# Where a filler's steps stand at the ends of the RWKV mixer's pairs of heads

## The chip, the cores and the metric

The kernel runs on 1 core of one Trainium2 chip. The metric is the device time of one execution in microseconds. A core has TensorE (PE in the rows, PEld for its weight loads), VectorE (DVE), ScalarE (ACT), GpSimd (POOL) and SyncE (SP), which issues most of the DMAs. Each engine works through its own queue in the order that the program gives it.

## The reference

Two blocks of a network run over 512 tokens of width 1024. The first mixes the tokens in three branches (RWKV-7, S5, gated linear attention), weighs each with a gate, and goes on to cross-attention and a feed-forward part; the second has attention, a linear recurrence and two more feed-forward parts. The change lies in the RWKV branch, which has 8 heads of width 64. Cut to what matters:

```python
def step(S, inp):                                   # per token and head
    r_t, w_t, k_t, v_t, kk_t, a_t = inp
    sa = jnp.einsum('bhvk,bhk->bhv', S, -kk_t)
    S = (S * w_t[:, :, None, :] + sa[..., None] * (kk_t * a_t)[:, :, None, :]
         + v_t[..., None] * k_t[:, :, None, :])
    return S, jnp.einsum('bhvk,bhk->bhv', S, r_t)
_, y = lax.scan(step, S0, seq)
mean = jnp.mean(y, axis=-1, keepdims=True)
var = jnp.mean(jnp.square(y - mean), axis=-1, keepdims=True)
y = ((y - mean) * lax.rsqrt(var + RWKV_GN_EPS)).reshape(B, L, MIX_W) * ln_w + ln_b
bonus = jnp.sum(r_h * k_h * r_k, axis=-1, keepdims=True) * v_h
y = (y + bonus.reshape(B, L, MIX_W)) * g
...
gates = jax.nn.sigmoid(p_gate).reshape(B, L, N_BRANCH, D_MODEL)
merged = (gates[:, :, 0] * (y_rw @ w_branch[l, 0]) + gates[:, :, 1] * (y_s5 @ w_branch[l, 1])
          + gates[:, :, 2] * (y_gla @ w_branch[l, 2]))
```

## The kernel before

All matrices are multiplied in two parts, a high and a low one: one 128x128 weight block costs three matmuls of 512 columns. A weight tile of 512 KB is loaded by SP (`Stream.load`, L191; three raw buffers), split by ACT (L206) and VectorE (L207) into high and low halves (four buffers of half a tile each), and used.

The RWKV branch treats its 8 heads as four pairs, `hp` 0 to 3, each with 128 features. For a pair it projects k, r and v (`project`, 24 matmuls on L244 each; those of the next pair are traced at three places inside the present one, after the matrices of the pair, after the solve and before the loop). It then makes the pair's *front* (decays, normalised keys, transposes, the products NR, KR and A), *solves* a triangular system in chunks of 64 tokens (five rounds of 64x64 matmuls, L527, each with copies by ACT and sums by VectorE), computes UA, RT, GT and H, and goes through a *loop over chunks* (L719 to L729): each turn multiplies GT by the state, VectorE adds H (L724), and RT times the state gives the chunk's y. Behind the loop stands the *end of the pair*: VectorE adds the y's (L730), a matmul takes each head's mean away (L738, "the means"), ACT squares the result (L740), eight small matmuls sum the squares (L743, a helper on L349, "the sums"), VectorE, GpSimd and VectorE make reciprocal roots, four matmuls broadcast them (L744, on L366), and two more matmuls (L747 bonus, L752 gate) and VectorE finish the pair. The solve of a pair uses the same PSUM banks as the end of the pair before it.

Beside this runs the *filler* (`gates`, L1186): a generator whose every step is three matmuls of 512 columns on L1200. Eight steps make one tile: 16 tiles of gates for the merge of the branches, then 4 tiles of products for S5, 160 steps in all. They accumulate in one PSUM bank of their own; the eighth step of a tile ends with a tanh or a copy by ACT and a store to DRAM (for S5 nine stores, eight of them by SP, L1219). `b.fill(n)` traces the next n steps at its place; `b.fill_behind(ins, n)` traces them there too and makes their TensorE instructions come behind `ins` on TensorE's queue.

The order of every queue is set when the kernel is built. The planner takes, whenever an engine is free in its own reckoning, the instruction traced earliest among those whose operands are ready. So the place where a loose step is traced says only what goes before it when both are ready; a step can run far earlier than its neighbours in the code. For pairs 0 to 2 the code traces 3 steps in the front, 5 before NR, 16 in the solve, 6 in the loop and 2 behind it, 32 a pair, all loose. Pair 3 has 41 loose ones up to its solve and 23 tied ones: two behind each of six turns of the loop, then 3, 3 and 5 behind the last turn, the means and the sums.

Of the kernel before, what the change touches and what calls it, by code (L numbers as in the profile page):

```python
# [23 lines left out]
NCH = 8  # L24
# [452 lines left out]
def rwkv(b, st, xs, Y0, pp, ps, ctx, early):  # L477

    nc, v, c = b.nc, b.v, b.c
# [39 lines left out]
    def ch(t):  # L519
        return t.rearrange("p (c s) -> p c s", s=C64)  # L520

    def mmc(out, lhsT, rhs, cs=range(NCH), start=True, stop=True):

        for ci in cs:
            for a in range(2):
                r = slice(a * 64, a * 64 + 64)
                ins = nc.tensor.matmul(out(r, ci), lhsT(r, ci), rhs(r, ci), start=start, stop=stop)  # L527
        return ins

    def first():  # L530
        return pp.tile([P, 512], F32, tag="ps", name="pp")

    def bank():
        return ps.tile([P, 512], F32, tag="ps", name="ps")
# [3 lines left out]
    def work(name, pool=None):  # L538
        return (pool or w1).tile([P, L], F32, tag=tags.get(name, name), name=name)
# [16 lines left out]
    for hp in range(4):  # L556
# [21 lines left out]
        sq = work("sq")  # L578
        nc.scalar.activation(sq, k, AF.Square, scale=v["rw_k_k"][:, hp : hp + 1])
        b.fill(3)  # L580
        acc = first()
# [132 lines left out]
        y = work("y")  # L714
# [4 lines left out]
        for ci in range(1, NCH):  # L719
            prev = (lambda r, _: H[r, 0]) if ci == 1 else (lambda r, _: S[r, ci])  # L720
            if ci < NCH - 1:
                p = bank()[:, :C64]
                ins = mmc(lambda r, _: p[r], lambda r, _: GT[r, ci], prev, [0])
                nc.vector.tensor_tensor(S[:, ci + 1], H[:, ci], p, op=ALU.add)  # L724
            if hp == 3 and ci < NCH - 1:
                b.fill_behind(ins, 2)
            ins = mmc(lambda r, ci: py[r, ci], prev, lambda r, ci: RT[r, ci], [ci])
            if hp < 3 and ci < NCH - 1:
                b.fill()  # L729
        nc.vector.tensor_tensor(ch(y)[:, 1:], ch(y)[:, 1:], py[:, 1:], op=ALU.add)  # L730


        behind = (lambda ins, n: b.fill_behind(ins, n)) if hp == 3 else (lambda ins, n: None)
        if hp < 3:
            b.fill(2)
        behind(ins, 3)
        pc = bank()
        behind(nc.tensor.matmul(pc, c["cmat"], y, start=True, stop=True), 3)  # L738
        yc, sq = work("yc"), work("sq2")
        nc.scalar.activation(sq, pc, AF.Square)  # L740
        nc.scalar.copy(yc, pc)
        acc = bank()
        behind(b.token_sums(acc, sq, c["hsel"], 4, True, True), 5)  # L743
        rb = b.head_rows(acc[:, :8], ps, w1, 1.0 / 64, 64e-5, ("yr", "y"))  # L744
        nc.vector.tensor_tensor(yc, yc, rb, op=ALU.mult)
        pb = bank()
# [640 lines left out]
def block1(b, st, ctx, c0, context):  # L1387
# [6 lines left out]
    with ExitStack() as mx:  # L1394
# [18 lines left out]
        with ExitStack() as c:  # L1413
            Y0 = b.pool("yr", 1, ctx=c, side="right").tile([P, 4, L], F32, name="Y0")
            with ExitStack() as c1:
                b.filler = gates(b, st, hs, (2, 1), made, b.pool("gate", 1, ctx=c1), b.pool("ps1a", 1, PSUM, ctx=c1))
                rwkv(b, st, hs, Y0, b.pool("ps1p", 2, PSUM, ctx=c1), b.pool("ps1r", 3, PSUM, ctx=c1), c1, pre.make)
                b.drain()
            yp = room("ys")
            y0 = yp()  # L1420
            for k in range(4):
                b.scaled_parts(y0[0][:, k], y0[1][:, k], Y0[:, k], 0.5)
# [846 lines left out]
```

## Time and profile before

| | us |
|---|---|
| median of 3 runs | 3179.24 |
| lowest, highest | 3174.16, 3182.07 |
| the profiled execution's own time | 3181.27 |
| its span, first to last instruction | 3179.5 |
| TensorE busy in it | 3071.8 |
| RWKV's pairs in it | from about 40 to 400 us of the span |

The rows come from the profiled execution, in microseconds from its first instruction. Busy time of matmuls is modelled: they overlap, so the start of one to the start of the next says what one costs. A granted clock of 1.00 is 2.4 GHz, of 0.50 is 1.2 GHz.

### The profile page before, as it was taken

The numbers are of one execution on the slowest core, as the hardware profiler recorded it, in microseconds if no ns is written. First come the engines' busy times: TensorE is split into PE (matmuls) and PEld (weight loads), VectorE is DVE, ScalarE is ACT, GpSimd is POOL, SyncE is SP. The second block draws the span as 40 slices with busy tenths as digits, with TensorE's granted clock in tenths as the row PEclk, the third lists the DMA queues.
The fourth block names the chain that finished last, engine by engine and source line by source line (L and its number), as shares of the span: only waits on it lengthen the run. The fifth ranks groups of instructions, "written<-read, shape, count | busy, mean of one in ns | idle before, by whom it ended". The sixth has DMA issues, their size and how long they took to land.

```text
span 3179.5 us, 51627 instructions
## 1 busy us (share of the span) xinstructions
PE 3071.8 (97%) x20456; PEld 2635.5 (83%) x20456; DVE 1841.7 (58%) x3374; ACT 1247.0 (39%) x2436; POOL 748.5 (24%) x827
## 2 busy tenths in 40 slices
PE   8999899989999999899999999999999999899998
PEld 6888777769797888896669988888999998788888
DVE  6545395556465556777767784323655656653445
ACT  4333234335354334646655221212544444332323
POOL 3322141220030000568765000000322223210002
PEclk9999999999999999999999999999999999999999
DMA  4122233334154332432225473221421111123334
GB/s 141 59 74 65 68 96 90 123 100 139 54 170 143 119 99 84 144 97 81 80 75 166 145 262 98 61 66 58 134 73 54 49 59 47 47 75 98 95 97 120
DMA packets 115938, 310.29 MB, mean 98 GB/s; under 512 B 32352, under 2 KB 37168, under 8 KB 115184
## 3 DMA queue, kind: packets, MB, share of 16 engines
q1 hardware_dynamic: 110480, 294.99, 30.0%
q10 hardware_dynamic: 5216, 12.00, 1.0%
q8 instruction: 161, 2.64, 0.3%
q14 instruction: 81, 0.66, 0.1%
HBM read 296.23 MB, written 9.44 MB: 96 GB/s over the span
## 4 chain that ended last, share of the span: by engine, by line
PE 86%; DVE 8%; issue 2%; POOL 2%; DMA 1%; ACT 1%; SPq 0%; DVEq 0%; POOLq 0%; ACTq 0%
PE acc L244 58%; PE gate L1200 3%; PE ps L527 3%; PE acc L265 2%; PE acc L267 2%; PE acc L266 2%; PE ps L1998 2%; DVE wl L207 2%; PE mods L1508 1%; PE ss L349 1%; PE rstd L425 1%; PE sc L1763 1%; PE st L1784 1%; PE acc L1806 1%; PE st L1785 1%
## 5 line engine op out<-in xcount | busy, mean ns | idle before, releaser
L206 ACT CAST wh<-raw 128x512 fp32r<-128x512 f32 (+1 forms) x899 | 538.1, 604 | 836.5 <-PE acc L244 662.9
L207 DVE TENSOR_TENSOR wl<-raw,wh 128x512 fp32r<-128x512 f32 (+1 forms) x779 | 578.4, 745 | 494.5 <-ACT wh L206 491.3
L244 PE MATMUL acc<-hh,wl 128*128 128x512 f32 (+2 forms) x2264 | 747.7, 363 | 9.3 <-DVE th L1236 4.4
L244 PE MATMUL acc<-hh,wh 128*128 128x512 f32 (+2 forms) x2264 | 747.3, 361 | 0.0
L244 PE MATMUL acc<-hl,wh 128*128 128x512 f32 (+2 forms) x2264 | 746.7, 361 | 0.0
L244 PEld LDWEIGHTS acc<-hh,wl 128*128 128x128 f32 (+1 forms) x2264 | 396.6, 189 | 84.3 <-issue 5.2
L244 PEld LDWEIGHTS acc<-hh,wh 128*128 128x128 f32 (+1 forms) x2264 | 397.3, 189 | 67.4 <-issue 1.9
L244 PEld LDWEIGHTS acc<-hl,wh 128*128 128x128 f32 (+1 forms) x2264 | 396.6, 189 | 63.8 <-issue 0.6
L207 POOL TENSOR_TENSOR wl<-raw,wh 128x512 fp32r<-128x512 f32 (+1 forms) x120 | 142.9, 1193 | 1106.8 <-ACT wh L206 1097.3
L244 PE MATMUL acc<-mh,wl 128*128 128x512 f32 (+1 forms) x848 | 262.2, 335 | 1.2 <-DVE wl L207 0.8
L244 PE MATMUL acc<-mh,wh 128*128 128x512 f32 (+1 forms) x848 | 260.4, 332 | 0.0
L244 PE MATMUL acc<-ml,wh 128*128 128x512 f32 (+1 forms) x848 | 260.2, 331 | 0.1
L244 PEld LDWEIGHTS acc<-mh,wl 128*128 128x128 f32 x848 | 150.5, 188 | 18.3 <-DVE wl L207 1.2
L244 PEld LDWEIGHTS acc<-ml,wh 128*128 128x128 f32 x848 | 150.8, 188 | 17.7 <-DVE ml L343 0.5
L244 PEld LDWEIGHTS acc<-mh,wh 128*128 128x128 f32 x848 | 150.5, 188 | 17.2
L354 POOL TENSOR_TENSOR rs<-rs,ct_all 128x2 f32<-128x2 f32 (+1 forms) x32 | 27.5, 860 | 449.3 <-DVE rs L416 449.3
L265 PE MATMUL acc<-wl,hh 128*128 128x256 f32 x448 | 126.5, 285 | 1.4 <-DVE Xc L1574 1.4
L266 PE MATMUL acc<-wh,hl 128*128 128x256 f32 x448 | 126.6, 284 | 0.0
L267 PE MATMUL acc<-wh,hh 128*128 128x256 f32 x448 | 125.7, 284 | 0.0
L1574 DVE SCALAR_TENSOR_TENSOR X<-acc,mod,X 128x256 f32<-128x256 f32 (+1 forms) x112 | 65.2, 593 | 94.8 <-PE acc L244 94.6
L1622 ACT ACTIVATE t<-acc 128x512 f32<-128x512 f32 x66 | 34.6, 526 | 195.1 <-PE acc L244 195.1
L1794 POOL TENSOR_TENSOR pl<-pr,ph 128x512 fp32r<-128x512 f32 x75 | 103.0, 1382 | 9.4 <-ACT ph L1791 4.5
(604 smaller groups left out, 5826.0 us busy)
## 6 DMA issues: line engine op xcount, KB each, us to landing
raw<-in_ffn_in_dram SPq DMA_DIRECT2D x88, 512.0 KB, 3.6
ada<-in_ada_dram SPq DMA_DIRECT2D x48, 512.0 KB, 3.8
w<-in_ada_dram SPq DMA_DIRECT2D x48, 512.0 KB, 4.5
raw<-in_ffn_w_up_dram SPq DMA_DIRECT2D x44, 512.0 KB, 3.6
raw<-in_ffn_out_dram SPq DMA_DIRECT2D x32, 512.0 KB, 3.5
raw<-in_hg_w_dram SPq DMA_DIRECT2D x32, 512.0 KB, 3.5
raw<-in_ffn_out_dram SPq DMA_DIRECT2D x40, 384.0 KB, 3.1
raw<-in_w_gate_dram SPq DMA_DIRECT2D x24, 512.0 KB, 3.6
```

Source lines behind the costliest of these rows:

```text
L206: nc.scalar.copy(h, x)
L207: (nc.gpsimd if self.help and n else nc.vector).tensor_tensor(l, x, h.bitcast(F32), op=ALU.subtract)
L244: nc.tensor.matmul(z[0], w, z[x], start=k == 0 and n == 0, stop=k == ks - 1 and n == 2)
L265: nc.tensor.matmul(acc, xh, wl, start=k == 0, stop=False)
L266: nc.tensor.matmul(acc, xl, wh, start=False, stop=False)
L267: nc.tensor.matmul(acc, xh, wh, start=False, stop=k == ks - 1)
L527: ins = nc.tensor.matmul(out(r, ci), lhsT(r, ci), rhs(r, ci), start=start, stop=stop)
L1200: nc.tensor.matmul(acc, w, x, start=k + i == 0, stop=k == 7 and i == 2)
L1574: return lambda i, acc: b.nc.vector.scalar_tensor_tensor(X[:, i], acc, gate[:, i : i + 1], X[:, i], op0=ALU.mult, op1=ALU.add)
L1622: nc.scalar.activation(t, a, AF.Tanh, scale=0.5)
L1794: (nc.vector if n % 3 == 1 else nc.gpsimd).tensor_tensor(pl, pr, ph.bitcast(F32), op=ALU.subtract)
L1998: nc.tensor.matmul(p[:, c], kc[:, c * P : (c + 1) * P], qc[:, c * P : (c + 1) * P], start=True, stop=True)
```

## The change

For pairs 0 to 2 the loop traces three loose steps instead of six, one in each of the turns 1, 3 and 5; the two loose steps behind the loop go; two steps are tied behind the means and three behind the sums. A pair still has 32 steps, and pair 3 keeps its ties as they are.

```diff
             ins = mmc(lambda r, ci: py[r, ci], prev, lambda r, ci: RT[r, ci], [ci])
-            if hp < 3 and ci < NCH - 1:
-                b.fill()
+            if hp < 3 and ci % 2:
+                b.fill((1, 1, 1, 0)[ci // 2])
         nc.vector.tensor_tensor(ch(y)[:, 1:], ch(y)[:, 1:], py[:, 1:], op=ALU.add)
 
 
-        behind = (lambda ins, n: b.fill_behind(ins, n)) if hp == 3 else (lambda ins, n: None)
-        if hp < 3:
-            b.fill(2)
-        behind(ins, 3)
+        if hp == 3:
+            b.fill_behind(ins, 3)
         pc = bank()
-        behind(nc.tensor.matmul(pc, c["cmat"], y, start=True, stop=True), 3)
+        b.fill_behind(nc.tensor.matmul(pc, c["cmat"], y, start=True, stop=True), 3 if hp == 3 else 2)
...
         acc = bank()
-        behind(b.token_sums(acc, sq, c["hsel"], 4, True, True), 5)
+        b.fill_behind(b.token_sums(acc, sq, c["hsel"], 4, True, True), 5 if hp == 3 else 3)
```

## Rows read from the trace of the kernel before

**Rows 1.** The page: busy time of engines (share, instructions); a load's us to landing.
```profile
PE 3071.8 (97%) x20456; PEld 2635.5 (83%) x20456; DVE 1841.7 (58%) x3374; ACT 1247.0 (39%) x2436; POOL 748.5 (24%) x827
...
raw<-in_w_gate_dram SPq DMA_DIRECT2D x24, 512.0 KB, 3.6
```

**Rows 2.** Stretches: length, busy time of each engine (instructions), granted clock, DMA share, GB/s.
```profile
270.60:324.40 53.80, 53.49 (x925) 45.72 (x925) 30.04 (x55) 17.09 (x37) 16.07 (x19) 1.00 0.20 61
324.40:341.10 16.70, 11.24 (x83) 7.07 (x77) 3.99 (x12) 1.66 (x3) 1.65 (x1) 0.69 0.01 2
341.10:365.90 24.80, 23.02 (x709) 22.12 (x708) 10.29 (x22) 6.06 (x14) 3.77 (x6) 1.00 0.01 3
```

**Rows 3.** Stretches, the filler's line L1200 alone: its matmuls, then its weight loads.
```profile
40.00:97.50 57.50, 18.19 (x72) 13.31 (x73) 1.00 0.31 97
97.50:181.50 84.00, 30.84 (x120) 21.58 (x120) 1.00 0.21 64
181.50:270.60 89.10, 35.23 (x142) 26.07 (x142) 1.00 0.22 72
270.60:329.50 58.90, 20.49 (x78) 13.85 (x77) 1.00 0.18 56
329.50:365.90 36.40, 0.00 (x0) 0.00 (x0) 0.86 0.01 3
```

**Rows 4.** Timeline of TensorE at pair 0's end.
```profile
181.51 1.10 PE L738 MATMUL ps<-y,ct_mix 128*128 128x512 f32 x2
...
187.49 0.95 PE L349 MATMUL ps<-ct_mix,sq 128*128 128x2 f32 x8
...
195.19 1.05 PE L366 MATMUL hb<-ct_all,hw 128*128 128x128 f32 x8
196.07 1.02 PE L747 MATMUL ps<-rk,bsel 128*128 128x512 f32 x2
```

**Rows 5.** Timeline of TensorE in pair 0's loop (start, duration, engine, line, operation).
```profile
152.28 0.39 PE L1200 MATMUL gate<-hl,wh 128*128 128x512 f32 x1
152.60 0.33 PE L527 MATMUL ps<-S,GT 64*64 64x64 f32 x4
152.97 0.50 PE L1200 MATMUL gate<-hh,wh 128*128 128x512 f32 x1
153.31 0.39 PE L1200 MATMUL gate<-hh,wl 128*128 128x512 f32 x1
153.54 0.40 PE L1200 MATMUL gate<-hl,wh 128*128 128x512 f32 x1
```

**Rows 6.** Timeline of TensorE at pair 2's end, with idle time and what ended it.
```profile
329.57 2.02 PE L738 MATMUL ps<-y,ct_mix 128*128 128x512 f32 x2 [0.79 <-DVE y L730]
332.34 1.86 PE L349 MATMUL ps<-ct_mix,sq 128*128 128x2 f32 x8 [0.75 <-ACT sq L740]
336.74 2.04 PE L366 MATMUL hb<-ct_all,hw 128*128 128x128 f32 x8 [2.54 <-DVE hw L363]
338.58 1.68 PE L747 MATMUL ps<-rk,bsel 128*128 128x512 f32 x2
```

**Rows 7.** Stretches of 3 us at pair 2's end, columns as in rows 2.
```profile
330.00:333.00 3.00, 2.25 (x6) 0.68 (x5) 0.00 (x0) 1.07 (x2) 0.00 (x0) 0.50 0.00 0
...
336.00:339.00 3.00, 2.26 (x9) 2.21 (x10) 0.53 (x2) 0.00 (x0) 0.13 (x1) 0.50 0.00 0
```

**Rows 8.** Loops of pairs 0 and 2: all engines, then twice L527 alone.
```profile
149.00:178.20 29.20, 29.20 (x193) 21.82 (x188) 10.13 (x19) 10.70 (x18) 6.66 (x8) 1.00 0.25 77
...
149.00:178.20 29.20, 3.75 (x86) 2.78 (x80) 1.00 0.25 77
...
324.40:328.70 4.30, 2.92 (x59) 2.06 (x53) 1.00 0.01 3
```

**Rows 9.** Dense work after a fall of the clock, columns as in rows 2.
```profile
690.00:695.00 5.00, 4.85 (x12) 3.83 (x13) 3.07 (x4) 0.63 (x1) 1.66 (x1) 0.51 0.31 97
```

**Rows 10.** Timelines: SP's stores for S5, TensorE in pair 3's loop.
```profile
316.65 5.32 SPq L1219 DMA_DIRECT2D scr<-gate  x8
...
371.96 0.33 PE L527 MATMUL ps<-S,GT 64*64 64x64 f32 x4 [2.10 <-DVE S L724]
```

## The prediction

> **What bounds the kernel now.** I began with the page: TensorE is busy 97% of the span [rows 1]. The change moves no arithmetic, so only three things can alter the time here: TensorE waiting, TensorE at its lower clock, and the small loss each time it passes between 64x64 and 128x128 tiles. Next I read stretches of the mixer. Up to 324.4 us TensorE has no gap worth naming (53.49 of the last 53.80 us busy); from 324.40 to 341.10 it is busy 11.24 of 16.70 us at a granted clock of 0.69, and in the next 24.80 us it is busy 23.02 [rows 2]. I call the four pairs of heads 0 to 3; these two stretches are the loop over chunks and the end of pair 2, and then pair 3's solve.
>
> Why it waits there is in the count of the filler's matmuls (three to a step) [rows 3]. 72+120 = 192 of them, 64 steps, are done when pair 0's means start at 181.51 [rows 4], though only 32 steps are written in the code up to there. At pair 1's means it is 111 against 64, and at pair 2's means 137 against 96. Between 329.5 and 365.9 there is none: what is left are the 23 steps that the code ties behind pair 3's matmuls. So loose steps run whenever TensorE's queue has room, long before the place where they are written, and they are used up when pair 2 ends.
>
> **The change, part by part.** It keeps 32 steps for each of pairs 0 to 2: three loose ones in the loop (there were six, and two behind it), two tied behind the means, three behind the sums of squares. A tie is an order on TensorE's queue and no semaphore; but the filler is one sequence into one PSUM bank, so no later step can pass a tied one. The means of pairs 0, 1 and 2 will then have at most 27, 59 and 91 steps before them, where they have 64, 111 and 137. That is 37, 52 and 46 steps later; 46 steps are 138 matmuls of about 0.23 us (153.31 to 153.54 [rows 5]), 31.7 us of work that pair 2's end and pair 3's solve don't have now.
>
> *Gain at pair 2's end.* The sums wait 0.75 us for the squares and the broadcast of the reciprocal roots waits 2.54 us [rows 6]. Two steps (1.4 us) stand behind the means and three (2.1 us), then 41 loose ones, behind the sums, so both waits are filled: -3.3 us. TensorE's clock is 0.50 from 330 to 339 us, its 1.2 GHz level, after the sparse loop [rows 6, 7]; means, sums, broadcast and bonus take 2.02+1.86+2.04+1.68 = 7.60 us there and 1.10+0.95+1.05+1.02 = 4.12 us at pair 0's end at 2.4 GHz [rows 4, 6]: -3.5 us. Bounds for both together: -6.8 and 0 (0 if the clock and the waits only change place).
>
> *Pair 3's solve.* 1.78 us of waits [rows 2] could be filled. But a visit of filler to the small matmuls is not free. In pair 0's loop a large matmul starts at 152.28, eight small ones at 152.60, the next large ones at 152.97 and 153.31: 0.69 us for one large (0.23) and eight small (8 x 0.03), 0.22 too much, and 0.11 more on the next start, so 0.33 us per visit [rows 5]. Five rounds with one visit each give back 1.65 us. I take 0, between -1.8 and +1.7.
>
> *Loss at the loops of pairs 0 and 1.* Step 24 is reached at 97.5 us [rows 3], so step 27 comes before pair 0's solve, and its loop will be bare as pair 2's is now. Pair 0's loop lasts 29.20 us and holds 193 matmuls, 86 of them small (2.5 us) and 107 large (24.6 us at 0.23): some 2 us are lost, as six visits of 0.33 us are. The bare loop of pair 2 takes 4.30 us for 59 small ones (1.7 us): 2.6 us lost [rows 8]. Losing the cover costs only 0.6 us a loop. Behind the loop the means wait for the sum of y, 0.79 us [rows 6]; the tied steps stand behind the means and can't fill it. 1.4 us a pair, +2.8 us for two; bounds 0 (a late projection still covers them) and +6.4 (both solves bare too, at the 1.78 us of pair 3's).
>
> The Trainium skill, page "TensorEngine Tiling (Array Packing)", section "Key Properties", says that a change of tiling mode drains TensorE. The 0.33 us per visit agrees [rows 5]; by that rule alone each loop that loses its filler would come out even, and the sum would be 1.2 us lower.
>
> *Clock at the three ends.* A bare loop was followed by the low clock once, at pair 2; the covered ones never (1.00 [rows 3, 8]). All three ends are bare now, but dense filler follows the means. Where dense work follows elsewhere, the clock reads 0.51 for some five microseconds with TensorE busy 4.85 of 5 [rows 9], about 2.5 us lost a fall. Bounds 0 and 3 x 3.5 = 10.5; I take the value near the low end, a fall or less in three, +2.0 us.
>
> *What moves with the steps.* Each gate tile's loads on SP, its casts on ACT, its subtractions on VectorE, and its tanh and store on the ACT queue. Pair 2's tile of products for S5 goes with them: its eight stores hold SP 5.32 us from 316.65 [rows 10], and will stand later, ahead of the next weight loads. I count 0, as three raw buffers are loaded ahead and TensorE has other tied work; if one load lies open it is 3.6 us [rows 1]. Two half-used gate tiles keep the four weight slots until the sums, so pair 2's first projection, written behind the second of them, waits for pair 0's sums; nothing of pairs 0 and 1 reads it before. Behind a tied step on TensorE's queue stands whatever comes later in the program; nothing of the chain waits for a step.
>
> *Sum.* -3.3 -3.5 +2.8 +2.0 = -2.0 us. The profiled execution took 3181.27 us (span 3179.5), 2.0 us above the median of the runs, 3179.24; the runs differ by 8 us. On the median: 3177.
>
> **The rivals.**
> *More than that* (faster). The clock holds at all three ends, the loops keep projections as cover, the solve's 1.78 us and the 2.10 us that pair 3's loop waits for VectorE [rows 10] go: -6.8-1.8-2.1 = -10.7 us, 3168.5. For it: 46 steps then lie where none do. Against: the 2.10 us hang on a load for S5 (VectorE's queue), not on missing filler, and pair 0 runs dry at 97.5 us.
>
> *The holes go from one end to three* (slower). Before, one pair was bare; after, three are. If each end has its fall as long as pair 2's now: 3 x 3.5 - 3.5 = +7.0; -3.3 for the waits; +2.8 for loops and y; and pair 0's solve, 32 filler matmuls poorer, finds pair 1's front not ready and waits 2.54 + 1.78 us as pair 2's end and pair 3's solve do: +4.3. With 1 us for the late stores that is +11.8, 3191. It decides where the clock stays at 0.5 for more than six microseconds behind each of the three means. For it: the one bare loop did that. Against: a busy queue follows at once.
>
> The Trainium skill, page "TensorE: Matmul & The Clock Gate", section "HAM oscillation — how this bites in real kernels", has this as a rule: a loop that leaves TensorE waiting on each pass falls to half rate on each pass, and every pass begins cold. The trace shows it once, at pair 2 [rows 7].
>
> *The order hardly changes* (3179): the steps would have landed there anyway. Against: 64 steps now lie ahead of pair 0's means.
>
> **How the numbers follow.** A measurement of this kernel can tell about 0.3%, 9.5 us, from no change. My forecast 0.62, more than that 0.18, holes at three ends 0.15, no change of order 0.05. The forecast's own range is 3170 to 3185 (unknown casts, and the runs' 8 us); with the rivals 3166 to 3192. Faster by over 0.3%: most of the second case and little of the first, 0.19; slower: 0.16; within: 0.65.
>
> **What would show it.** Filler matmuls before the three means at most 81, 177 and 273, and over a hundred between pair 2's means and pair 3's loop; the sums and the broadcast of pair 2 without waits over 0.3 us, its means at about 1.1 us; VectorE's y ahead of an idle of some 0.8 us in pairs 0 to 2; pair 3's loop beginning 0 to 7 us earlier than 365.97. I am wrong if pair 0's solve shows waits of several microseconds, if the clock stays low behind two or more ends, or if the gain is there at 366 us and gone when pair 3 ends.

## The result and the profile after

| kernel | median, us | lowest, highest | runs |
|---|---|---|---|
| after | 3203.57 | 3197.64, 3206.39 | 6 |
| before, beside it | 3177.86 | 3173.25, 3182.07 | 6 |

The ratio is 1.0074, interval [1.0063, 1.0086]: the change makes the kernel slower by 25.7 us. The forecast was 3177.0 in a range of 3166 to 3192, so both miss. The profiled execution after the change took 3206.39 us (span 3204.6), 25.1 more than the one before.

**Where the time went.** From the timeline of TensorE I take every matmul from 40 us to the end of pair 3's bonus (the same 480 of the filler, 295 of projections and 3408 small 64x64 ones in both), and its time from its start to the next one's. From this I take off what the same matmul takes in dense work (0.2275 us for 512 columns, 0.029 for a small one, 0.059 where it has 128 columns), and what TensorE shows as idle. The rest I put to the low clock where the granted clock is 0.50, and else to "the rest", nearly all of which is lost where TensorE goes between small and other tiles. Cut at the means, in us:

| stretch up to | idle before, after | low clock | rest |
|---|---|---|---|
| means of pair 0 | 0.0, 6.2 | 0.0, 2.8 | 9.1, 7.4 |
| means of pair 1 | 0.2, 4.3 | 0.0, 2.1 | 3.7, 8.0 |
| means of pair 2 | 2.5, 2.8 | 0.0, 1.6 | 4.3, 7.0 |
| means of pair 3 | 8.0, 4.7 | 3.3, 3.1 | 5.0, 8.3 |
| all, with pair 3's end | 10.7, 18.0 | 3.3, 9.6 | 22.3, 30.8 |

That is 7.3 + 6.3 + 8.5 = 22.1 us of the 22.2 by which the mixer is longer. Pairs 0, 1 and 2 lose 7.3, 10.5 and 4.6 us; pair 3, for which the gain was forecast, stays within 0.2. The stage after the mixer starts 22.2 us late, and the last 3 us come and go later (in a second execution of the same kernel the delay was 24.3 us here and 23.5 at the end).

The first view after is the filler's matmuls (now on L1198) by stretch, the second those of the projections (L244) in the first two stretches; columns as in [rows 3].

```profile
40.00:97.50 57.50, 18.22 (x72) 1.00 0.30 97
97.50:146.30 48.80, 2.20 (x9) 0.94 0.05 13
146.30:235.40 89.10, 26.38 (x96) 0.98 0.18 55
235.40:320.50 85.10, 26.38 (x96) 0.98 0.18 57
320.50:386.00 65.50, 37.85 (x139) 0.97 0.24 74
```
```profile
40.00:97.50 57.50, 30.75 (x129) 1.00 0.30 97
97.50:146.30 48.80, 0.26 (x2) 0.94 0.05 13
146.30:235.40 89.10, 18.56 (x72) 0.98 0.18 55
```

For comparison the projections before the change, from 97.5 us to pair 0's means:

```profile
97.50:181.50 84.00, 19.67 (x73) 1.00 0.21 64
```

The filler stands as forecast: 81, 177 and 273 matmuls before the three means, and 139 more up to 386 us, where pair 3's loop begins. But between 97.5 us and pair 0's means there are only 9 of them, and only 2 of projections. Before the change it was 120 [rows 3] and 73: not only the filler is missing in pair 0's solve, but also the projections, which then come one pair later. The way is the weight slots: after the change ACT splits no weight tile (L206) from 99.0 to 149.75 us, where before it splits six, and the next split stands behind a matmul of the tied filler:

```profile
149.75 0.62 ACT L206 CAST wh<-raw 128x512 fp32r<-128x512 f32 x1 [0.21 <-PE gate L1198]
```

The waits of TensorE in the mixer (line waited at, what it waited for: us in total, times, longest):

```profile
PE ps L527 <- DVE S L724: 7.4, 8, 3.3
PE hb L366 <- DVE hw L363: 3.3, 2, 3.0
...
PE pp L527 <- DVE KR L641: 1.5, 2, 0.7
PE ps L527 <- DVE RT L701: 0.7, 1, 0.7
...
PE ps L527 <- DVE T L683: 0.6, 1, 0.6
```

The longest of each kind in the timelines of TensorE (start, duration, operation, in brackets the idle time before it), with the instruction of VectorE that stands in the way of one of them. First the broadcast in pair 1's front, which runs inside pair 0's solve, and pair 0's end:

```profile
109.30 1.75 PE L366 MATMUL hb<-ct_all,hw 128*128 128x128 f32 x8 [3.01 <-DVE hw L363]
...
146.36 2.08 PE L736 MATMUL ps<-y,ct_mix 128*128 128x512 f32 x2 [0.79 <-DVE y L730]
147.44 1.42 PE L1198 MATMUL gate<-hh,wl 128*128 128x512 f32 x1
148.66 0.63 PE L1198 MATMUL gate<-hl,wh 128*128 128x512 f32 x1
149.08 0.63 PE L1198 MATMUL gate<-hh,wh 128*128 128x512 f32 x1
```

Then pair 1's loop, and VectorE there:

```profile
231.71 0.28 PE L527 MATMUL ps<-RT,S 64*64 64x64 f32 x4
234.37 0.33 PE L527 MATMUL ps<-RT,S 64*64 64x64 f32 x4 [2.38 <-DVE S L724]
235.49 1.62 PE L736 MATMUL ps<-y,ct_mix 128*128 128x512 f32 x2 [0.79 <-DVE y L730]
```
```profile
232.98 1.23 DVE L568 TENSOR_TENSOR_SCAN cum<-ct_mix,s 128x512 f32<-128x512 f32 x1 [2.26 <-POOL s L566]
234.12 0.20 DVE L724 TENSOR_TENSOR S<-H,ps 128x64 f32<-128x64 f32 x1
```

The state's sum takes VectorE 0.20 us, but stands behind pair 2's scan, which waits for GpSimd. Such a queue can cost nothing while TensorE has other work, and here it has none. Pair 2's end, which answers to [rows 6], and pair 3's loop, which answers to [rows 10]:

```profile
320.54 1.33 PE L736 MATMUL ps<-y,ct_mix 128*128 128x512 f32 x2 [0.80 <-DVE y L730]
324.23 1.19 PE L349 MATMUL ps<-ct_mix,sq 128*128 128x2 f32 x8
327.96 1.13 PE L366 MATMUL hb<-ct_all,hw 128*128 128x128 f32 x8 [0.34 <-DVE hw L363]
328.93 1.02 PE L745 MATMUL ps<-rk,bsel 128*128 128x512 f32 x2
...
393.00 0.48 PE L527 MATMUL ps<-S,GT 64*64 64x64 f32 x4 [3.29 <-DVE S L724]
```

Pair 2's waits are gone but for 0.34 us. The low clock there is shorter, 3.3 us against 10.2, and has come up in other places. In five stretches of the mixer the granted clock is 0.50 (columns as in [rows 2], TensorE alone):

```profile
109.70:113.10 3.40, 3.40 (x38) 0.50 0.02 5
143.90:150.60 6.70, 5.70 (x27) 0.50 0.01 2
236.00:239.40 3.40, 3.40 (x8) 0.50 0.00 0
321.40:324.70 3.30, 3.30 (x10) 0.50 0.00 0
393.00:396.40 3.40, 3.40 (x12) 0.50 0.00 0
```

Each comes in or right behind a wait or a bare loop. Inside them a filler matmul starts 0.42 us after the one before (148.66 to 149.08) where it is 0.23 at 2.4 GHz. The Trainium skill, page "TensorE: Matmul & The Clock Gate", section "HAM oscillation — how this bites in real kernels", describes a loop in which TensorE waits on each pass, for a DMA there, and each pass begins cold. The trace agrees in kind: here TensorE waits mostly for VectorE, in every pair, and has some 20 us at 1.2 GHz in the mixer, against 10.2 before.

Last, a piece of pair 1's solve, where projections now visit the small matmuls:

```profile
186.21 0.63 PE L527 MATMUL ps<-Z,Y 64*64 64x64 f32 x16
186.77 0.50 PE L244 MATMUL acc<-hh,wl 128*128 128x512 f32 x1
187.11 0.39 PE L244 MATMUL acc<-hl,wh 128*128 128x512 f32 x1
...
187.80 0.40 PE L244 MATMUL acc<-hl,wh 128*128 128x512 f32 x1
188.13 0.68 PE L527 MATMUL ps<-Y,Z 64*64 64x64 f32 x16
188.74 0.49 PE L244 MATMUL acc<-hh,wh 128*128 128x512 f32 x1
```

Sixteen small ones take 0.47 us in dense work, and a large one 0.23. Here it is 0.56 (186.21 to 186.77), 0.34, 0.33 and 0.61: about 0.1 us more on each side of a change of tile shape. Up to pair 3's end TensorE's queue has 132 such changes, before it had 90.

### The profile page after: what moved, and what is told of

Same layout as the page of the kernel before. It is cut to its first block, busy times and chain, and to the rows that moved or that the text cites. A ratio compares the mean times of both kernels' runs of the same rounds, so it can differ in the third digit from the quotient of the medians.

```text
span 3204.6 us, 51610 instructions
## 1 busy us (share of the span) xinstructions
PE 3088.0 (96%) x20456; PEld 2644.6 (83%) x20456; DVE 1838.5 (57%) x3374; ACT 1246.6 (39%) x2436; POOL 752.1 (23%) x827
## 4 chain that ended last, share of the span: by engine, by line
PE 85%; DVE 8%; POOL 2%; issue 2%; DMA 2%; ACT 2%; SPq 0%; DVEq 0%; POOLq 0%; ACTq 0%
PE acc L244 58%; PE gate L1198 4%; PE ps L527 3%; PE acc L265 2%; PE acc L266 2%; PE acc L267 2%; PE ps L1996 2%; DVE wl L207 1%; PE mods L1506 1%; PE ss L349 1%; PE rstd L425 1%; PE sc L1761 1%; DVE y L438 1%; PE st L1782 1%; PE acc L1804 1%
## 5 line engine op out<-in xcount | busy, mean ns | idle before, releaser
L206 ACT CAST wh<-raw 128x512 fp32r<-128x512 f32 (+1 forms) x899 | 538.1, 604 | 858.7 <-PE acc L244 662.6
L244 PE MATMUL acc<-hh,wl 128*128 128x512 f32 (+2 forms) x2264 | 746.4, 362 | 9.9 <-DVE th L1234 4.2
L244 PE MATMUL acc<-hl,wh 128*128 128x512 f32 (+2 forms) x2264 | 745.5, 361 | 0.0
L244 PE MATMUL acc<-hh,wh 128*128 128x512 f32 (+2 forms) x2264 | 744.9, 360 | 0.0
L244 PEld LDWEIGHTS acc<-hh,wl 128*128 128x128 f32 (+1 forms) x2264 | 395.5, 189 | 82.3 <-DVE th L1234 4.7
L244 PEld LDWEIGHTS acc<-hh,wh 128*128 128x128 f32 (+1 forms) x2264 | 396.5, 189 | 67.7 <-issue 1.9
L244 PEld LDWEIGHTS acc<-hl,wh 128*128 128x128 f32 (+1 forms) x2264 | 396.6, 189 | 63.2 <-issue 0.4
L244 PE MATMUL acc<-mh,wl 128*128 128x512 f32 (+1 forms) x848 | 261.2, 334 | 1.2 <-DVE wl L207 0.8
L244 PE MATMUL acc<-mh,wh 128*128 128x512 f32 (+1 forms) x848 | 260.1, 331 | 0.0
L244 PE MATMUL acc<-ml,wh 128*128 128x512 f32 (+1 forms) x848 | 259.9, 331 | 0.1
L244 PEld LDWEIGHTS acc<-mh,wl 128*128 128x128 f32 x848 | 150.1, 188 | 18.4 <-DVE wl L207 1.2
L244 PEld LDWEIGHTS acc<-mh,wh 128*128 128x128 f32 x848 | 150.9, 188 | 17.1
L244 PEld LDWEIGHTS acc<-ml,wh 128*128 128x128 f32 x848 | 150.4, 188 | 17.1 <-DVE ml L343 0.3
L1792 POOL TENSOR_TENSOR pl<-pr,ph 128x512 fp32r<-128x512 f32 x75 | 101.7, 1365 | 11.8 <-ACT ph L1789 5.9
```

Source lines behind the costliest of these rows:

```text
L206: nc.scalar.copy(h, x)
L244: nc.tensor.matmul(z[0], w, z[x], start=k == 0 and n == 0, stop=k == ks - 1 and n == 2)
L1792: (nc.vector if n % 3 == 1 else nc.gpsimd).tensor_tensor(pl, pr, ph.bitcast(F32), op=ALU.subtract)
```

## The experiments

All times are medians; the ratio is to the kernel before on the same chip. "Lost" is idle + low clock + rest in the mixer, as above (before 10.7 + 3.3 + 22.3, after 18.0 + 9.6 + 30.8).

| kernel | us, runs | ratio, interval | filler matmuls before the three means | projections before pair 0's means | changes of shape | lost |
|---|---|---|---|---|---|---|
| pair 0 tied | 3192.52, 6 | 1.0048 [1.0035, 1.0060] | 81/261/406 | 127 | 106 | 13.1 + 11.3 + 25.1 |
| pair 1 tied | 3189.24, 7 | 1.0029 [1.0018, 1.0039] | 177/177/358 | 199 | 110 | 11.5 + 11.1 + 25.4 |
| pair 2 tied | 3193.34, 6 | 1.0049 [1.0038, 1.0061] | 192/273/273 | 199 | 102 | 14.2 + 11.8 + 22.4 |
| quota | 3197.75, 6 | 1.0062 [1.0049, 1.0076] | 177/318/396 | 126 | 144 | 13.8 + 6.4 + 33.5 |
| one step | 3212.16, 4 | 1.0100 [1.0087, 1.0114] | 93/189/285 | 150 | 140 | 17.9 + 18.6 + 29.9 |
| block | 3202.57, 6 | 1.0074 [1.0061, 1.0087] | 81/177/273 | 126 | 116 | 22.2 + 11.1 + 28.5 |
| reserve 8 | 3180.15, 12 | 1.0006 [0.9998, 1.0015] | 192/336/387 | 198 | 84 | 7.8 + 3.2 + 20.9 |
| reserve 16 | 3181.85, 12 | 1.0004 [0.9995, 1.0014] | 192/336/363 | 198 | 84 | 8.4 + 6.2 + 20.3 |
| reserve 8, loop | 3178.36, 12 | 0.9995 [0.9984, 1.0005] | 192/336/375 | 198 | 82 | 7.0 + 4.8 + 20.3 |

The theory that I tested: a tie costs little itself, but the filler is one sequence, so a tied step holds back every step behind it (and through the weight slots the projections behind it); the barrier empties the solves before it, and the held work comes back as visits to the small matmuls behind it. The rival: each tied place has a price of its own.

**The change at one pair alone.** The edit for pair 0; for the others `hp == 1`, `hp == 2`:

```diff
-            if hp < 3 and ci < NCH - 1:
+            if hp == 0 and ci % 2:
+                b.fill((1, 1, 1, 0)[ci // 2])
+            if hp < 3 and hp != 0 and ci < NCH - 1:
                 b.fill()
...
+        tied = hp in (0, 3)
+        ins = nc.tensor.matmul(pc, c["cmat"], y, start=True, stop=True)
+        if tied:
+            b.fill_behind(ins, 3 if hp == 3 else 2)
...
+        ins = b.token_sums(acc, sq, c["hsel"], 4, True, True)
+        if tied:
+            b.fill_behind(ins, 5 if hp == 3 else 3)
```

> The change at pair 0 alone; pairs 1 and 2 as before. Barrier theory (a tied step holds every later one, so pair 0's solve and loop run dry): the means of pair 0 stand behind 81 filler matmuls instead of 192, its solve, loop and end lose some 10 us (about 6 of waits, 5 of low clock, less what the covered solve lost on switches), and pair 2's end stays as it was: +8 to +12 us against before. Clock theory (only the falls at the ends cost): +4 to +6 us, with the waits small. Tie theory (steps in the queue between the means and the sums delay the end, wherever the barrier lies): a third of the whole, +8, but then the quota kernel loses as well.

> The change at pair 1 alone. 177/177/358 filler matmuls before the means of pairs 0/1/2, so that pair 1's solve and loop run without filler; 110 shape changes. Barrier theory: like the change at pair 2 alone, whose bare pair lost 3.5 us more in waits and 8.5 us more at the low clock: +10 to +15, 3188 to 3193. Rival, the three places add up to the change (+25.7 with +14.2 at pair 0 and +15.0 at pair 2): -3.5, 3175.

> The change at pair 2 alone; pairs 0 and 1 as before. Barrier theory: 273 filler matmuls are gone before pair 1's means and none is left until pair 2's means, so solve and loop of pair 2 are bare (about +3 of waits), pair 2's end is filled (-3.3) and its low clock shorter (-2), but pair 3's solve then changes between small and large matmuls some 10 times (+3): 0 to +6 us against before. Clock theory: -2 to 0. Tie theory: +8.

Against the kernel before beside them (3178.36, 3180.54, 3178.36) the three cost 14.2, 8.7 and 15.0 us. Together that is 37.9, and the whole change costs 25.7, so the places don't add up, as if one barrier did part of the next one's harm. The theory had the direction and not the sizes: it gave 8 to 12, 10 to 15 and 0 to 6. At pair 2 it counted some 3 us of waits and left out the low clock, which takes 8.5 us more in the mixer than before. With pair 2 tied there is no filler at all in its stretch, and TensorE waits there, at the end of pair 1 too:

```profile
259.25 2.05 PE L366 MATMUL hb<-ct_all,hw 128*128 128x128 f32 x8 [1.28 <-DVE hw L363]
263.69 1.05 PE L349 MATMUL ps<-ct_mix,sq 128*128 128x2 f32 x8 [0.69 <-ACT sq L745]
268.73 2.04 PE L366 MATMUL hb<-ct_all,hw 128*128 128x128 f32 x8 [3.99 <-DVE hw L363]
```

**One step.** Of the whole change only the last step of each pair is tied, behind the sums:

```diff
         if hp < 3:
-            b.fill(2)
+            b.fill(1)
...
-        behind(b.token_sums(acc, sq, c["hsel"], 4, True, True), 5)
+        b.fill_behind(b.token_sums(acc, sq, c["hsel"], 4, True, True), 5 if hp == 3 else 1)
```

> Before, but with one filler step (the last of the eight) tied behind the sums of squares of each of pairs 0 to 2, in place of the change's five in other places. The queue has 93/189/285 filler matmuls before the means of pairs 0/1/2 (81/177/273 after the change, 192/334/411 before it) and 140 changes between the small and the large tile shape (132 and 90). Barrier theory (one tied step holds back every later step of the filler's list, so the number of tied steps hardly matters): +20 to +28 us on before, 3198 to 3206. Rival, each tied step has its own price: a fifth of the change's +25, about +5, 3183.

It is 31.6 us slower, more than the change itself and six times the rival's 5: three tied steps instead of fifteen, and no less harm. So what costs is not the number of ties; the barrier fits. Its own 20 to 28 was too low: the low clock takes 18.6 us here, perhaps as nothing stands behind the means, which no run separates. The filler's matmuls between 97.5 us and pair 0's means:

```profile
97.50:155.20 57.70, 4.85 (x21) 0.96 0.07 21
```

**Quota.** The change's ties, but more of the loose steps in early pairs (59, 42, 21 and 0), so that the barrier holds back little filler:

```diff
...
-            b.fill((4, 3, 3, 3, 3)[i] if hp < 3 else 7 if i else 5)
+            b.fill(((12, 9, 9, 9, 9), (7, 6, 6, 6, 6), (2, 2, 2, 2, 2), (0,) * 5)[hp][i])
```

> The ties of the changed kernel at all three pairs, but the loose steps moved: 59, 42 and 21 before the three means instead of 27 each, none in pair 3's front and solve, so that the barriers stand about where the kernel before had come by itself (177, 318 and 396 filler matmuls before the means, 192, 334 and 411 in the kernel before). Barrier theory: most of the loss goes; what stays is the projections that wait for weight slots, and 144 changes of tile shape against 90 before: 0 to +8 us against before. Tie theory: as slow as the changed kernel, +20 to +25. Clock theory: falls at the ends stay as they are in the changed kernel, +7.

It was 19.4 us slower, not 0 to 8: here my number failed, and the rival's 20 to 25 came nearest, though one step, above, and the reserve, below, speak against it. The filler's counts are near those of before, but the projections are not: 126 before pair 0's means, as few as after the change (127), where before had 199, and 72 in each of the next two stretches. Its rest is 33.5 us, with 144 changes of shape. So filler held back is not the whole; the weights are loaded in the order of the code, and moving filler ahead or tying it moves the projections behind it. This run changes both orders at once, so the share of the projections alone stays open; more weight slots would have told it and weren't tried.

**Block.** The change's ties, and the loose steps of pairs 1 to 3 tied in one block behind the end of the pair before:

```diff
...
-        nc.tensor.matmul(pg, gup[:, hp * P : hp * P + P], sgd, start=True, stop=True)
+        ins = nc.tensor.matmul(pg, gup[:, hp * P : hp * P + P], sgd, start=True, stop=True)
+        if hp < 3:
+            b.fill_behind(ins, 24 if hp < 2 else 41)
```

> The change's ties, and besides, the loose steps of pairs 1 to 3 (24, 24 and 41) tied in one block behind the end of the pair before, so that these pairs' solves and loops run bare and the filler runs dense between them. 81/177/273 filler matmuls before the means as after the change, 116 shape changes against 132. Theory that the visits of filler to a solve cost as much as they hide: a bare pair lost 13.6 us beside its work in the run with pair 2 alone tied, 4.0 of which the wait for the sums that the block now covers, so 9.6 against the change's 11.4, 14.4 and 16.1 in pairs 2, 1 and 3 (idle, low clock and the rest): 8 to 13 us less than after the change, 3191 to 3196. Rival, the filler in the solves hides waits at next to nothing and a bare solve costs more: the same or slower than after the change, 3203 to 3212.

The same as after the change (3202.57 and 3203.57), so the theory that visits cost as much as they hide, which had 8 to 13 us less, falls. The 16 changes of shape fewer give 2.3 us of rest back, but idle time grows by 4.2 and the low clock by 1.5. Filler that runs dense elsewhere and leaves the solve bare is no better than filler in the solve.

**Reserve.** All steps loose but the last 8 (3 and 5) or 16 (3 and 13) of pair 3's own loose ones, which are tied behind pair 2's means and sums. Nothing stands behind them in the sequence but pair 3's own ties, so they hold nothing back:

```diff
...
-            b.fill((4, 3, 3, 3, 3)[i] if hp < 3 else 7 if i else 5)
+            b.fill((4, 3, 3, 3, 3)[i] if hp < 3 else 0)
...
-            b.fill(2)
+            b.fill(2 if hp < 2 else 35)
...
+        if hp == 2:
+            b.fill_behind(ins, 3)
...
+        if hp == 2:
+            b.fill_behind(ins, 5)
```

> No ties at pairs 0 and 1; 3 steps tied behind pair 2's means and 5 behind its sums, taken from pair 3's loose ones, all other loose steps written before pair 2's means. Barrier theory: the barrier stands at step 129 of 137, so nothing before it runs dry earlier by more than 8 steps; the waits of 0.75 and 2.54 us at pair 2's end go and the low clock there is shorter: -3 to -7 us against before. Clock theory: about the same, -2 to -4. Tie theory: +2 to +4.

> All steps loose but 16 of pair 3's own, which are tied behind pair 2's means (3) and sums of squares (13): nothing stands behind them in the list, so nothing is held back. 192/336/363 filler matmuls before the means, 84 shape changes against 90 before. In the run with 8 such steps the mixer ended 4.7 us sooner than before, and 5.3 us were lost again between 440 and 520 us, where the granted clock fell for 13.7 us at 485 and before it had not. Theory that this loss goes with the earlier arrival: the clock falls there again, 3177 to 3181. Rival, it fell there by chance in that one execution: -4 to -6 us, 3172 to 3175.

With 8 the waits of pair 2's end are gone, as meant, and TensorE's timeline shows both without one; the low clock at the end remains (2.08 us for the means):

```profile
323.15 2.08 PE L738 MATMUL ps<-y,ct_mix 128*128 128x512 f32 x2 [0.79 <-DVE y L730]
...
328.60 0.95 PE L349 MATMUL ps<-ct_mix,sq 128*128 128x2 f32 x8
...
332.55 1.13 PE L366 MATMUL hb<-ct_all,hw 128*128 128x128 f32 x8
```

The mixer ends 4.7 us sooner, so these eight ties, with nothing behind them, do no harm in it, unlike the one step a pair above. But the kernel is no faster, against the 3 to 7 us expected: the gain is given back between 440 and 520 us. Second executions of three kernels were to tell whether that was chance:

> The kernel before, unchanged, for a second profiled execution. In its first one the granted clock fell for 10.2 us in the mixer (at 329.66) and not between 400 and 570 us, where it fell in seven of the nine other profiled kernels (477 to 499). If the clock's falls are fixed by the queue, they come at the same places again; if they differ by execution, one comes in this stretch in some executions of the kernel before, and the gain of 8 reserved steps (4.7 us up to the mixer's end) was not lost by arriving sooner.

> The 8 reserved steps again, for a second profiled execution. Its mixer should end 4 to 7 us sooner than before's by the waits and the shape changes (idle 7.8 and rest 20.9, against 10.7 and 22.3); if the clock's fall at 485 us is fixed by the earlier arrival, it is there again, else it may be missing.

> The kernel after, unchanged, for a second profiled execution. Theory of waits: up to the mixer's end the idle time is again 18 us (17 to 19), and so is the rest at the full clock (30 to 32); the loss at the low clock, 9.6 us in the first execution, may differ by some us.

With 16 the kernel takes 3181.85 us, just above the 3177 to 3181 of the theory that the loss comes again, and far from the 3172 to 3175 of chance. For this fall it is hardly chance. The stage at 480 to 500 us, first in the kernel before, again (3179.81 us), then with 8 steps reserved, again (3180.01):

```profile
480.00:490.00 10.00, 6.83 (x37) 1.00 0.32 106
490.00:500.00 10.00, 10.00 (x68) 1.00 0.53 134
```
```profile
480.00:490.00 10.00, 6.59 (x37) 0.82 0.34 109
490.00:500.00 10.00, 10.00 (x42) 0.50 0.37 84
```

In all four executions with reserved steps the clock falls at 485 to 489 us for 13.7 us; in neither execution of before it does. At 480 us the projections of the second one with 8 steps were 5.2 us ahead of those in the first one of before, at 520 us 2.4 behind. Other falls do differ between executions of one kernel: the second one of before has one of 6.8 us at 400.7 us, which the first has not. The second execution of after, 3204.77 us, lost 17.4 + 13.1 + 29.7 us in the mixer: idle time and rest repeat within 1.1 us (the rest just under the 30 expected), the low clock differs by 3.5.

**Reserve 8, loop.** Four more of pair 3's steps tied where its loop waits 3.0 us for S:

```diff
             if hp == 3 and ci < NCH - 1:
-                b.fill_behind(ins, 2)
+                b.fill_behind(ins, 6 if ci == 1 else 2)
```

> The 8 reserved steps, and 4 more of pair 3's own 41 loose ones tied behind the first matmuls of pair 3's loop, where the run with 8 waited 3.0 us for the state S. 375 filler matmuls before pair 2's means, 82 shape changes. Theory of waits: the 3.0 us go, and the mixer ends 2 to 3 us sooner than with 8; over the whole kernel 3174 to 3179. Rival, the low clock takes it back wherever the small matmuls then run alone (pair 3's solve has no filler left): no difference from before, 3179 to 3182.

The mixer does not end the 2 to 3 us sooner that the theory of waits had: 1.9 us of the wait are left, the low clock takes 1.6 us more, as the rival said, and the mixer ends where it did with 8. The clock falls at 486.6 us again. The time, 3178.36, lies in the theory's range and not in the rival's, but from before (3179.53 beside it) no difference can be told. No run gave a version that is measurably faster than the kernel before.

## Why the prediction was wrong

*Right.* The order: at most 81, 177 and 273 filler matmuls before the means, exactly so, and over a hundred in pair 3's solve. At pair 2's end the sums don't wait and the broadcast waits 0.34 us: 2.95 of the 3.3 us of the term. That idle time up to pair 3's means falls by just 3.3 us is partly luck, as waits in pair 3's solve and loop changed too. y is waited for 0.79 to 0.80 us in pairs 0 to 2.

*The step that failed* is "Loss at the loops of pairs 0 and 1": +2.8 us, with a bound of +6.4 for "both solves bare too". The stretches up to the means of these two pairs lose 17.8 us more, and pair 2's, which had no term, 4.6; without the low clock, which has its own term below, that is 12.9 and 3.0. I priced the loops and left out what the missing filler does to the solves, though the text itself found pair 0's solve dry. Measured: in pair 0's solve TensorE waits 3.01 us for pair 1's front and 0.64 + 0.73 us for the solve itself; pair 1's loop waits 0.75 + 2.38, since VectorE's queue holds the next pair's front there; and the rest grows by 4.3 and 2.7 us in pairs 1 and 2.

*"What moves with the steps ... I count 0"* failed with it. The prediction saw that pair 2's projections would wait for pair 0's sums, and called it free, as nothing reads them before. It forgot that they were cover: 73 matmuls between 97.5 us and pair 0's means became 2, and they came back as visits in the next pairs.

*"Pair 3's solve": 0, between -1.8 and +1.7.* The idle time there went down a little, but 26 more changes of shape cost 3.3 us: not five rounds with one visit each, but thirteen. Over all 14 profiled executions the rest is 4.2 us + 0.196 us for each change, within 1.8 us. That is 0.39 us for a visit, against the 0.33 read from [rows 5]; the price was nearly right and the count wrong. These counts differ together with much else, so the line is a fit and no test.

*"Clock at the three ends": +2.0 us.* Measured, for the mixer, +6.3 in the profiled execution and +9.8 in the second, within the bound of 10.5 but three to five times the value taken. The argument that dense filler follows the means at once did not save it: it runs at 1.2 GHz itself (147.44 to 150.36). And the -3.5 us of the gain at pair 2's end came to nothing, as the low clock in pair 3's stretch (3.3, now 3.1 us) moved in part to its loop. Low clock behind two or more ends, and waits of several microseconds in pair 0's solve, were two of the prediction's own signs of being wrong; both came.

*Pair 3's loop* began at 385.8 us, where 359 to 366 was expected. Its wait for S rose from 2.10 to 3.29 us; that part of the argument held, since VectorE stands there behind S5's product, idle for 4.60 us until its load lands, after the change as before.

*The rival* "the holes go from one end to three" named the mechanism and came to +11.8. Its low clock (+7.0), pair 0's solve (+4.3; 4.4 measured) and pair 2's waits (-3.3) were near; it had no changes of shape (+8.5) and too little for pair 1. It deserved the larger chance: "a busy queue follows at once" was the only thing against it.

## What to carry to other kernels

A tie in a sequence that can't be overtaken is a barrier: count what stands behind it, here some 40 to 50 steps and the projections that share their weight slots, and ask what every stage before it will use as cover instead. Filler for a known hole is better taken from the end of the sequence, where nothing stands behind it; here that closed the hole without harm, though it gained nothing in the whole kernel. A queue without a gap hides the waits of all other engines; before work is taken out of one of its stages, that stage's own chain has to be priced, and not only the stage that is to get the work.

## What the runs showed of the hardware

The same gain can be lost by the clock in a stage that the change doesn't touch. With 8 steps reserved, second execution, TensorE waits 2.31 and 0.97 us in the stage at 480 us with only eight matmuls between, and then runs at 1.2 GHz (0.43 us from 487.94 to 488.37, two matmuls):

```profile
484.59 1.05 PE L1082 MATMUL ps<-Gm,bb 128*16 128x128 f32 x8 [2.31 <-ACT ET L1071]
486.61 0.69 PE L1134 MATMUL ps<-sx,Gm 128*128 128x64 f32 x2 [0.97 <-DVE sx L1131]
...
487.94 0.63 PE L1135 MATMUL ps<-U,toep 128*128 128x64 f32 x2
488.37 0.64 PE L1134 MATMUL ps<-sx,Gm 128*128 128x64 f32 x2
```

In the kernel before, again, the two waits are 1.67 and 1.51 us, and the clock stays at 1.00:

```profile
486.19 1.05 PE L1076 MATMUL ps<-Gm,bb 128*16 128x128 f32 x8 [1.67 <-ACT ET L1065]
489.40 0.43 PE L1128 MATMUL ps<-sx,Gm 128*128 128x64 f32 x2 [1.51 <-DVE sx L1125]
```

The idle time is the same within 0.1 us (3.28 and 3.18). In both executions of before two projections stand between the two waits, which had run earlier with 8 reserved. Arriving sooner is not what decides: with pair 2 alone tied TensorE comes to this stage 12 us later than before, also without projections between, and the clock falls at 498.8 us:

```profile
498.54 1.66 PE L1083 MATMUL ps<-Gm,bb 128*16 128x128 f32 x8 [2.31 <-ACT ET L1072]
500.55 0.69 PE L1135 MATMUL ps<-sx,Gm 128*128 128x64 f32 x2 [0.36 <-DVE sx L1132]
```

So it is in all five profiled executions without projections between these waits (this one and the four with reserved steps), and in none of the five that have them (before and after, twice each, and pair 0 tied; after and pair 0 tied come 13 to 24 us later than before). The order of the matmuls goes with the fall; that it causes it is only argued, as no run changes this order alone.
